# FFN-down of a hybrid decoder layer: 29 of 64 squares by seven products instead of 22, with the weight sums of 15 of them made ahead and kept in DRAM

## The chip, the cores and the metric

The kernel runs on one core of one Trainium2 chip. The metric is the device time of one execution in microseconds. Five engines matter: TensorE (PE, with its weight loads as PEld), VectorE (DVE), ScalarE (ACT), GpSimd (POOL) and SyncE (SP). SP computes nothing here; it issues nearly all DMAs, in order, and waits on semaphores.

## The reference, cut to what matters

The whole layer has 256 tokens and a width of 2048. The change touches only the channel mixer:

```python
h2 = rms_norm(x, mlp_norm[i])                                          # 256 x 2048
x = x + jnp.square(jax.nn.relu(h2 @ w_ffn_up[i])) @ w_ffn_down[i]      # 2048 -> 8192 -> 2048
gate = jax.nn.sigmoid(rms_norm(x, ple_norm[i]) @ w_ple_gate[i])        # comes next
```

All of it is float32. `w_ffn_up` and `w_ffn_down` have 64 MB each and are read once from DRAM.

## The kernel before, in words

**Precision.** Every float32 operand is split into a high part (rounded to `fp32r` by an ACT copy) and a low part (the rest, by a DVE subtraction). A product is then three matmuls: high by high, high by low, low by high. For a weight tile of 128x1024, `halves_of` (L1115 ff.) issues two ACT copies of 128x512 (L1122) and one DVE subtraction of 128x1024 (L1123). `split_sb` (L154, L155) does the same for one 128x512 block.

**Order in time.** `ffn_half(0)` and `ffn_half(1)` follow each other. Each one runs eight `gemm_wide` (the up half: 1024 of the 8192 hidden columns at a time in two `half` steps of 256 columns, 64 loads of 512 KB per up half) and then two `down_sweep`s, one for each `pair` (1024 of the 2048 output columns). A sweep goes over 16 values of `kp`; each is a "square": 256 hidden rows by 1024 output columns, by 256 tokens. Two halves, two sweeps and 16 squares make 64 squares.

**A square.** Its weights are two loads of 512 KB, `rx` and `ry`. With 128x512 blocks b11, b12 (`rx`) and b21, b22 (`ry`) and 128x128 blocks of activations a11 to a22, the plain form has eight block products of three matmuls each: 24 matmuls. The other form (`kp in seven`) is Winograd's with seven products: 21 matmuls, but it needs sums of the activations (`activation_sums`, made in the up half and kept in the `S` tiles) and sums of the weights. The weight sums t1, t3, t2, t4 are four DVE operations of 128x512 (L1151 to L1154) inside the sweep, into the tile `td` of slot `a1`, and are then split like weights. Before the change the seven-product squares are kp 1, 3, 6, 8, 11, 13, and only 1, 3, 6, 11 in the last sweep: 3 x 6 + 4 = 22.

**Buffers.** The pool `wp` has three slots of each of three tags: `raw` (what a DMA writes, 512 KB), `wh` and `wl` (the split halves that PE reads). All weight loads of the kernel share the three `raw` slots through `load_raw` (L138 to L140). The fourth split tile of a seven-product square is taken from the tag `graw` of the pool `fp`. `keep` loads four tiles of the gate weights in the last sweep (`graw` too), and the row of the final norm (`fn`) goes into slot `a0` when that is free.

**Who sets the order.** The code is written as a data flow. A scheduler in the compiler sets each engine's order of instructions before the run, by priority (program order, and ahead of it what stands in `tc.high_priority`) among the instructions whose inputs and slots are there by its own account. At run time each engine and SP's queue then go through that fixed order, and wait where they must.

Of the kernel before, what the change touches and what calls it, by code (L numbers as in the profile page):

```python
# [9 lines left out]
F32 = mybir.dt.float32  # L10
F32R = mybir.dt.float32r
AF = mybir.ActivationFunctionType
ALU = mybir.AluOpType
# [27 lines left out]
def trunk(  # L41
# [23 lines left out]
    act = ctx.enter_context(tc.tile_pool(name="act", bufs=1))  # L65
    psm = ctx.enter_context(tc.tile_pool(name="psm", bufs=4, space=PSUM))
    rctx = ctx.enter_context(ExitStack())
    psr = rctx.enter_context(tc.tile_pool(name="psr", bufs=4, space=PSUM))

    def mm_bank(name):  # L70
# [20 lines left out]
    make_identity(nc, ident)  # L91
    ones = const.tile([128, 128], F32, name="ones")
    nc.vector.memset(ones, 1.0)
    jsum = const.tile([128, 128], F32, name="jsum")
    cmask = const.tile([128, 128], F32, name="cmask")
    rmask = const.tile([128, T], F32, name="rmask")
    sbd = [const.tile([128, 4, 128], F32, name=f"sbd{i}") for i in range(2)]
    make_block_diagonal(nc, cmask, 64)
    nc.gpsimd.tensor_copy(jsum, cmask)
    cen = const.tile([128, 128], F32, name="cen")  # L100
    nc.vector.scalar_tensor_tensor(cen, jsum, -1.0 / 64.0, ident, op0=ALU.mult, op1=ALU.add)
    jhead = const.tile([128, 2], F32, name="jhead")
    nc.gpsimd.tensor_copy(jhead, cmask[:, ::64])
    for r0 in (0, 64):
        make_upper_triangular(nc, cmask[r0 : r0 + 64, 0:64], val=1.0, diag=False)
# [2 lines left out]
    nc.gpsimd.memset(rmask.rearrange("p (c t) -> p c t", t=64)[:, :, 0:1], 0.0)  # L108
    for i in range(2):
        nc.vector.memset(sbd[i], 0.0)  # L110
    edge = const.tile([128, 4, 16], F32, name="edge")
    nc.vector.memset(edge, 1.0)
    for g, win in enumerate(WINDOWS):
        for t in range(win - 1):
            nc.gpsimd.memset(edge[:, g, t : t + 1], float(win) / (t + 1))


    wband = const.tile([128, 4, 272], F32, name="wband")

    def make_bands():  # L120
        for g, win in enumerate(WINDOWS):
# [6 lines left out]
            nc.vector.tensor_tensor(w0[:, 0:128], w0[:, 0:128], ident, op=ALU.subtract)  # L128

    m0, m1 = PARAM_COLS["mu_r"], PARAM_COLS["mu_wag"] + 3  # L130
    omu = const.tile([128, m1 - m0], F32, name="omu")
    nc.vector.tensor_scalar(omu, par_sb[:, m0:m1], -1.0, 1.0, op0=ALU.mult, op1=ALU.add)
    oka = const.tile([128, 8], F32, name="oka")
# [4 lines left out]
    def load_raw(src, n, name):  # L138
        raw = wp.tile([128, 1024], F32, tag="raw", name=f"raw_{name}")
        nc.sync.dma_start(raw[:, 0:n], src)  # L140
        return raw
# [11 lines left out]
    def split_sb(h_ap, l_ap, src_ap):  # L153
        nc.scalar.activation(h_ap, src_ap, AF.Copy)  # L154
        nc.vector.tensor_tensor(l_ap, src_ap, h_ap.bitcast(F32), op=ALU.subtract)  # L155
# [93 lines left out]
    def a8(slot, name, dt=F32):  # L249
        return act.tile([128, 2048], dt, tag=f"a{slot}", name=name)  # L250
# [36 lines left out]
    hsel = const.tile([8, 512], F32R, name="hsel")  # L287
    nc.gpsimd.tensor_copy(hsel, hsel_f)

    def flat(t_):  # L290
# [89 lines left out]
    normed(0)  # L380
    normed(1)

    zf = const.tile([128, 3, T], F32, name="zf")
    zwa, zg, zg2 = zf[:, 0], zf[:, 1], zf[0:64, 2]

    def wag_out():
# [681 lines left out]

    SEVEN = (1, 3, 6, 8, 11, 13)
    s_slots = (0, 2, 5)

    def activation_sums(box, kp, r):

        i = SEVEN.index(kp)
        if i % 2 == 0:
            box[kp] = box[SEVEN[min(i + 1, len(SEVEN) - 1)]] = a8(s_slots[i // 2], f"S{kp}", F32R)
        st = box[kp][:, i % 2 * 1024 : i % 2 * 1024 + 1024]
        t_ = fp.tile([128, 1024], F32, tag="junk", bufs=1, name=f"s{kp}")  # L1080
        s1, s2_, s3, s4 = (t_[:, j * 128 : (j + 1) * 128] for j in range(4))
        a11, a21, a12, a22 = (r[:, j * 128 : (j + 1) * 128] for j in range(4))
        nc.vector.tensor_tensor(s1, a21, a22, op=ALU.add)
        nc.vector.tensor_tensor(s3, a11, a21, op=ALU.subtract)
        nc.vector.tensor_tensor(s2_, s1, a11, op=ALU.subtract)
        nc.vector.tensor_tensor(s4, a12, s2_, op=ALU.subtract)
        split_sb(st[:, 0:512], st[:, 512:1024], t_[:, 0:512])

    def down_sweep(hf, pair, ys, sboxes, hooks=(), between=None, seven=SEVEN):
# [43 lines left out]
        for q, kp in enumerate((0, 2, 1, 4, 3, *range(5, 16)) if pair else range(16)):  # L1133
            if q in hooks:
                hooks[q]()
            y, j = ys[kp // 2], kp % 2 * 512
            a11, a21, a12, a22 = ((y[:, j + i * 128 : j + i * 128 + 128], y[:, 1024 + j + i * 128 : 1152 + j + i * 128]) for i in range(4))
            rx, ry = (load_raw(w_down[pair, hf * 32 + 2 * kp + i], 1024, f"{nm}_{kp}_{i}") for i in range(2))
            if kp in seven:
                i = SEVEN.index(kp)  # L1140
                st = sboxes[kp][:, i % 2 * 1024 : i % 2 * 1024 + 1024]
                s1, s2_, s3, s4 = ((st[:, c * 128 : c * 128 + 128], st[:, 512 + c * 128 : 640 + c * 128]) for c in range(4))
                t_ = a8(1, f"t{nm}_{kp}")
                t1, t3, t2, t4 = (t_[:, c * 512 : c * 512 + 512] for c in range(4))
                wa = fp.tile([128, 1024], F32R, tag="wa", name=f"wa{nm}_{kp}")
                w11 = wa[:, 0:512], wa[:, 512:1024]
                with tc.high_priority(20000):
                    split_sb(*w11, rx[:, 0:512])
                w21, w22 = halves_of(ry, f"{nm}_{kp}b")
                with tc.high_priority(20000):  # L1150
                    nc.vector.tensor_tensor(t1, rx[:, 512:1024], rx[:, 0:512], op=ALU.subtract)  # L1151
                    nc.vector.tensor_tensor(t3, ry[:, 512:1024], rx[:, 512:1024], op=ALU.subtract)
                    nc.vector.tensor_tensor(t2, t3, rx[:, 0:512], op=ALU.add)
                    nc.vector.tensor_tensor(t4, ry[:, 0:512], t2, op=ALU.subtract)  # L1154
# [28 lines left out]
    def ffn_half(hf):  # L1183
        sboxes = {}
        ys = []
        for i in range(8):
            f = hf * 8 + i
            y = fp.tile([128, 2048], F32R, tag="y", bufs=8, name=f"y{f}")

            def square(bi, bank):  # L1190
                r = fp.tile([128, 512], F32, tag="r", bufs=2, name=f"r{f}_{bi}")
                r2 = r.rearrange("p (c t) -> p c t", c=2)
                nc.scalar.activation(r2, bank[:, :, T : 2 * T], AF.Copy)
                nc.vector.tensor_tensor(r2, bank[:, :, 0:T], r2, op=ALU.add)
                nc.vector.scalar_tensor_tensor(r, r, 0.0, r, op0=ALU.max, op1=ALU.mult)
                split_sb(y[:, bi * 512 : bi * 512 + 512], y[:, 1024 + bi * 512 : 1024 + bi * 512 + 512], r)
                if 2 * i + bi in SEVEN:
                    activation_sums(sboxes, 2 * i + bi, r)

            gemm_wide(w_up[f], h2, f"u{f}", square)  # L1200
            ys.append(y)
            if f == 1:
                inv_ms()

        if hf == 1:
            h3_part, h3 = transposed("h3")
            h3_box.append(h3)

        down_sweep(hf, 0, ys, sboxes)
        if hf == 0:  # L1210
            down_sweep(hf, 1, ys, sboxes)
        else:
            down_sweep(hf, 1, ys, sboxes, {5: keep, 8: keep, 11: keep, 14: keep}, lambda: [h3_part("ple_norm", n) for n in range(2)], (1, 3, 6, 11))
            for n in range(2, 4):
                h3_part("ple_norm", n)

# [149 lines left out]
```

## Time and profile before

| | us |
|---|---|
| median of 3 runs (lowest, highest) | 1203.55 (1201.89, 1203.93) |
| the profiled execution's own time | 1201.35 |
| its span in the profile | 1199.6 |

The mean granted TensorE clock of the profiled execution is 0.997. Its span lies 1.75 us under its own time, and its own time 2.2 us under the median. In the profile's rows, a group of instructions is given as line, engine, operation, what it writes and reads, count, busy time, and mean nanoseconds of one. `raw_d` are the loads of `w_ffn_down`, `raw_u` those of `w_ffn_up`; `d_b` and `d_w` are the PSUM banks of the down product, `u_w` of the up product; `wh_d_12a` and `wl_d_12a` are the split halves of a square's first load (kp 12), `b` the second, `c` and `d` the weight sums; `wad` is the split b11 block. A matmul's duration in a row is longer than its distance to the next, since matmuls are pipelined.

### The profile page before, as it was taken

The numbers are of one execution on the slowest core, as the hardware profiler recorded it, in microseconds if no ns is written. First come the engines' busy times: TensorE is split into PE (matmuls) and PEld (weight loads), VectorE is DVE, ScalarE is ACT, GpSimd is POOL, SyncE is SP. The second block draws the span as 40 slices with busy tenths as digits, with TensorE's granted clock in tenths as the row PEclk, the third lists the DMA queues.
The fourth block names the chain that finished last, engine by engine and source line by source line (L and its number), as shares of the span: only waits on it lengthen the run. The fifth ranks groups of instructions, "written<-read, shape, count | busy, mean of one in ns | idle before, by whom it ended". The sixth has DMA issues, their size and how long they took to land.

```text
span 1199.6 us, 18428 instructions
## 1 busy us (share of the span) xinstructions
PE 1179.5 (98%) x7060; PEld 1010.6 (84%) x7060; DVE 868.5 (72%) x1149; ACT 689.8 (58%) x1276; POOL 18.1 (2%) x69
## 2 busy tenths in 40 slices
PE   8999999999999999999999999999999999999997
PEld 6999988987887888888888788888888888777886
DVE  7687987965656666666878888666667879787552
ACT  6857566566545565555655564454555555668544
POOL 4000010000000000000000000000000000000000
PEclk9999999999999999999999999999999999999999
DMA  6463542354445555555665656655555556766531
GB/s 246 154 201 109 175 144 104 113 198 141 140 163 179 184 185 190 192 191 189 201 201 200 193 195 211 191 181 188 189 184 189 207 194 197 287 231 211 195 120 70
DMA packets 60328, 216.88 MB, mean 181 GB/s; under 512 B 6736, under 2 KB 7120, under 8 KB 59856
## 3 DMA queue, kind: packets, MB, share of 16 engines
q1 hardware_dynamic: 59952, 215.19, 53.4%
q8 instruction: 55, 0.90, 0.3%
q10 hardware_dynamic: 288, 0.52, 0.1%
q14 instruction: 33, 0.27, 0.1%
HBM read 213.59 MB, written 2.10 MB: 180 GB/s over the span
## 4 chain that ended last, share of the span: by engine, by line
PE 81%; DVE 8%; DMA 4%; ACT 4%; issue 2%; SPq 0%; ACTq 0%; DVEq 0%
PE u_w L997 20%; PE u_w L1001 10%; PE d_b L1112 5%; PE d_b L1113 5%; PE d_b L1111 5%; DMA raw_d<-in_w_ffn_down_dram 3%; PE gt_b L171 2%; PE gt_b L173 2%; PE gt_b L172 2%; PE wag_b L331 1%; PE zp_b L171 1%; PE o_b L171 1%; PE o_b L172 1%; PE o_b L173 1%; PE d_w L1112 1%
## 5 line engine op out<-in xcount | busy, mean ns | idle before, releaser
L997 PE MATMUL u_w<-h,wh_u 128*128 128x512 f32 x1024 | 358.8, 395 | 0.0
L1001 PE MATMUL u_w<-h,wl_u 128*128 128x256 f32 x1024 | 287.3, 281 | 0.0
L149 ACT ACTIVATE wh_u<-raw_u 128x512 fp32r<-128x512 f32 x256 | 147.6, 624 | 166.2 <-PE u_w L997 93.1
L150 DVE TENSOR_TENSOR wl_u<-raw_u,wh_u 128x1024 fp32r<-128x1024 f32 x128 | 156.7, 1225 | 115.1 <-ACT wh_u L149 115.1
L997 PEld LDWEIGHTS u_w<-h,wh_u 128*128 128x128 f32 x1024 | 192.0, 187 | 44.8
L1001 PEld LDWEIGHTS u_w<-h,wl_u 128*128 128x128 f32 x1024 | 193.6, 189 | 0.0
L150 DVE TENSOR_TENSOR wl_gt<-raw_gt,wh_gt 128x1024 fp32r<-128x1024 f32 x24 | 29.4, 1225 | 23.9 <-ACT wh_gt L149 23.9
L149 ACT ACTIVATE wh_gt<-raw_gt 128x512 fp32r<-128x512 f32 x48 | 27.8, 631 | 23.0 <-PE gt_b L173 18.8
L1151 DVE TENSOR_TENSOR td<-raw_d 128x512 f32<-128x512 f32 x22 | 15.2, 693 | 31.0 <-DMA raw_d<-in_w_ffn_down_dram 31.0
L162 PE MATMUL zv_b<-hTh,wh_zv 128*128 128x256 f32 x128 | 37.6, 294 | 0.0
L171 PE MATMUL gt_b<-wh_gt,h 128*128 128x512 f32 x96 | 37.5, 390 | 0.0
L162 PE MATMUL zr_b<-hTh,wh_zr 128*128 128x256 f32 x128 | 37.4, 292 | 0.0
L173 PE MATMUL gt_b<-wh_gt,h 128*128 128x512 f32 x96 | 37.4, 389 | 0.0
L172 PE MATMUL gt_b<-wl_gt,h 128*128 128x512 f32 x96 | 37.4, 389 | 0.0
L164 PE MATMUL zr_b<-hTh,wl_zr 128*128 128x256 f32 x128 | 37.0, 289 | 0.1
L163 PE MATMUL zr_b<-hTl,wh_zr 128*128 128x256 f32 x128 | 37.0, 289 | 0.0
L162 PE MATMUL zk_b<-hTh,wh_zk 128*128 128x256 f32 x128 | 36.9, 288 | 0.0
L163 PE MATMUL zk_b<-hTl,wh_zk 128*128 128x256 f32 x128 | 36.3, 284 | 0.5 <-DVE hTl L155 0.5
L164 PE MATMUL zk_b<-hTh,wl_zk 128*128 128x256 f32 x128 | 36.3, 284 | 0.1
L163 PE MATMUL zv_b<-hTl,wh_zv 128*128 128x256 f32 x128 | 36.2, 283 | 0.0
L164 PE MATMUL zv_b<-hTh,wl_zv 128*128 128x256 f32 x128 | 36.2, 283 | 0.0
L154 ACT ACTIVATE wad<-raw_d 128x512 fp32r<-128x512 f32 x22 | 13.9, 632 | 33.7 <-DMA raw_d<-in_w_ffn_down_dram 29.1
(807 smaller groups left out, 3077.6 us busy)
## 6 DMA issues: line engine op xcount, KB each, us to landing
raw_u<-in_w_ffn_up_dram SPq DMA_DIRECT2D x128, 512.0 KB, 3.6
raw_d<-in_w_ffn_down_dram SPq DMA_DIRECT2D x128, 512.0 KB, 4.0
raw_gt<-in_w_ple_gate_dram SPq DMA_DIRECT2D x24, 512.0 KB, 3.5
raw_zk<-in_w_in_dram SPq DMA_DIRECT2D x16, 512.0 KB, 3.3
raw_zr<-in_w_in_dram SPq DMA_DIRECT2D x16, 512.0 KB, 3.4
raw_zv<-in_w_in_dram SPq DMA_DIRECT2D x16, 512.0 KB, 3.2
raw_zp<-in_w_in_dram SPq DMA_DIRECT2D x16, 512.0 KB, 3.3
raw_o<-in_w_out_dram SPq DMA_DIRECT2D x16, 512.0 KB, 3.5
```

What stands on the lines that cost most here:

```text
L149: nc.scalar.activation(wh[:, a * 512 : (a + 1) * 512], raw[:, a * 512 : (a + 1) * 512], AF.Copy)
L150: nc.vector.tensor_tensor(wl, raw, wh.bitcast(F32), op=ALU.subtract)
L162: nc.tensor.matmul(o, w_h, ah, start=first and ct % 2 == 0, stop=False, skip_group_check=True)
L163: nc.tensor.matmul(o, w_h, al, start=False, stop=False, skip_group_check=True)
L164: nc.tensor.matmul(o, w_l, ah, start=False, stop=last, skip_group_check=True)
L171: nc.tensor.matmul(o, a_h, wh[:, 0:n], start=first, stop=False)
L172: nc.tensor.matmul(o, a_h, wl[:, 0:n], start=False, stop=False)
L173: nc.tensor.matmul(o, a_l, wh[:, 0:n], start=False, stop=last)
L997: nc.tensor.matmul(bank[:, ct, :].rearrange("p (s t) -> p s t", s=2), wh[:, c], hl, start=k == 0, stop=False, skip_group_check=True,)
L1001: nc.tensor.matmul(bank[:, ct, 0:T], wl[:, c], hl[:, 0, :], start=False, stop=k == 15, skip_group_check=True)
L1111: nc.tensor.matmul(banks[n], ah, wh, start=first, stop=False)
L1112: nc.tensor.matmul(banks[n], ah, wl, start=False, stop=False)
```

## The change

More squares take the seven-product form: kp 1, 3, 5, 7, 9, 11, 12, 13 in three sweeps and 1, 3, 7, 9, 11 in the last, 3 x 8 + 5 = 29. Of these, the squares with kp 3, 7, 11, 13 (3, 7, 11 in the last sweep), 15 in all, get their weight sums ahead of time: `ahead` loads both weight tiles in the up half before (2 x 512 KB), makes the four sums there with four DVE operations in place, and writes the 1 MB tile (t2, t1, t4, t3 in the places of b11, b12, b21, b22) to a DRAM scratch tensor `sums{n}`. The tile is in slot `a1` for odd n and in a new single slot `pr` for even n. The store of one tile is written in the code after the next `gemm_wide`.

In the sweep such a square reads four times instead of twice: 256 KB of `rx` (b11 alone), `ry`, and the two halves of the stored tile, all through the `raw` slots, and makes no sums. The other seven-product squares stay as they were. Two more pairs of activation sums are made per half, and a new tile `S` holds them. Constants that only the mixer needs move from the pool `const` to a pool `mixc` that is closed before the FFN, which gives the room for `pr` and `S`.

```diff
-    SEVEN = (1, 3, 6, 8, 11, 13)
+    SEVEN = (1, 3, 5, 7, 9, 11, 12, 13)
+    AHEAD = (3, 7, 11, 13)
+    LAST = (1, 3, 7, 9, 11)
     s_slots = (0, 2, 5)
+    sums = {}
+
+    def ahead(hf, pair, kp, n):
+        t_ = a8(1, f"pr{n}") if n % 2 else fp.tile([128, 2048], F32, tag="pr", name=f"pr{n}")
+        for i in range(2):
+            nc.sync.dma_start(t_[:, i * 1024 : (i + 1) * 1024], w_down[pair, hf * 32 + 2 * kp + i])
+        b11, b12, b21, b22 = (t_[:, c * 512 : c * 512 + 512] for c in range(4))
+        nc.vector.tensor_tensor(b22, b22, b12, op=ALU.subtract)
+        nc.vector.tensor_tensor(b12, b12, b11, op=ALU.subtract)
+        nc.vector.tensor_tensor(b11, b22, b11, op=ALU.add)
+        nc.vector.tensor_tensor(b21, b21, b11, op=ALU.subtract)
+        d = dram.tile([128, 2048], F32, name=f"sums{n}")
+        sums[hf, pair, kp] = d
+        return lambda: nc.sync.dma_start(d, t_)
...
-            rx, ry = (load_raw(w_down[pair, hf * 32 + 2 * kp + i], 1024, f"{nm}_{kp}_{i}") for i in range(2))
+            pre = kp in seven and sums.get((hf, pair, kp))
+            rx, ry = (
+                load_raw(w_down[pair, hf * 32 + 2 * kp + i][:, 0:n], n, f"{nm}_{kp}_{i}")
+                for i, n in enumerate((512 if pre else 1024, 1024))
+            )
...
+            if pre:
+                ra, rb = (load_raw(pre[:, c * 1024 : c * 1024 + 1024], 1024, f"{nm}_{kp}_t{c}") for c in range(2))
+                wa = fp.tile([128, 1024], F32R, tag="wa", name=f"wa{nm}_{kp}")
+                w11 = wa[:, 0:512], wa[:, 512:1024]
+                with tc.high_priority(20000):
+                    split_sb(*w11, rx[:, 0:512])
+                w21, w22 = halves_of(ry, f"{nm}_{kp}b")
+                w2, w1 = halves_of(ra, f"{nm}_{kp}c")
+                w4, w3 = halves_of(rb, f"{nm}_{kp}d", True)
+                for n, a_, w_ in (("1", a11, w11), ("2", a12, w21), ("3", s4, w22), ("5", s1, w1), ("6", s2_, w2), ("7", s3, w3), ("4", a22, w4)):
+                    prod(n, a_, w_)
+            elif kp in seven:
...
+        plan = [(pair, kp) for pair in range(2) for kp in AHEAD if kp in LAST or not (hf and pair)]
+        store = None
         for i in range(8):
             f = hf * 8 + i
+            stored, store = store, ahead(hf, *plan[i], hf * 8 + i) if i < len(plan) else None
...
             gemm_wide(w_up[f], h2, f"u{f}", square)
+            if stored is not None:
+                stored()
```

More of the change, by code (lines that the diff above doesn't have):

```diff
@@ L67, in trunk @@
     rctx = ctx.enter_context(ExitStack())
+    mixc = rctx.enter_context(tc.tile_pool(name="mixc", bufs=1))
+    dram = ctx.enter_context(tc.tile_pool(name="sums", bufs=1, space=bass.MemoryType.DRAM))
     psr = rctx.enter_context(tc.tile_pool(name="psr", bufs=4, space=PSUM))
@@ L93, in trunk @@
     nc.vector.memset(ones, 1.0)
[L94 to L97, printed above, removed]
+    jsum = mixc.tile([128, 128], F32, name="jsum")
+    cmask = mixc.tile([128, 128], F32, name="cmask")
+    rmask = mixc.tile([128, T], F32, name="rmask")
+    sbd = [mixc.tile([128, 4, 128], F32, name=f"sbd{i}") for i in range(2)]
     make_block_diagonal(nc, cmask, 64)
     nc.gpsimd.tensor_copy(jsum, cmask)
-    cen = const.tile([128, 128], F32, name="cen")
+    cen = mixc.tile([128, 128], F32, name="cen")
     nc.vector.scalar_tensor_tensor(cen, jsum, -1.0 / 64.0, ident, op0=ALU.mult, op1=ALU.add)
-    jhead = const.tile([128, 2], F32, name="jhead")
+    jhead = mixc.tile([128, 2], F32, name="jhead")
     nc.gpsimd.tensor_copy(jhead, cmask[:, ::64])
@@ L110, in trunk @@
         nc.vector.memset(sbd[i], 0.0)
-    edge = const.tile([128, 4, 16], F32, name="edge")
+    edge = mixc.tile([128, 4, 16], F32, name="edge")
     nc.vector.memset(edge, 1.0)
@@ L115, in trunk @@
             nc.gpsimd.memset(edge[:, g, t : t + 1], float(win) / (t + 1))
-    wband = const.tile([128, 4, 272], F32, name="wband")
+    wband = mixc.tile([128, 4, 272], F32, name="wband")
     def make_bands():
@@ L130, in trunk @@
     m0, m1 = PARAM_COLS["mu_r"], PARAM_COLS["mu_wag"] + 3
-    omu = const.tile([128, m1 - m0], F32, name="omu")
+    omu = mixc.tile([128, m1 - m0], F32, name="omu")
     nc.vector.tensor_scalar(omu, par_sb[:, m0:m1], -1.0, 1.0, op0=ALU.mult, op1=ALU.add)
-    oka = const.tile([128, 8], F32, name="oka")
+    oka = mixc.tile([128, 8], F32, name="oka")
     ka0 = PARAM_COLS["k_a"]
@@ L286, in trunk @@
     nc.gpsimd.affine_select(hsel_f, hsel_f, [[-1, 512]], ALU.is_ge, 0.0, base=63, channel_multiplier=64)
-    hsel = const.tile([8, 512], F32R, name="hsel")
+    hsel = mixc.tile([8, 512], F32R, name="hsel")
     nc.gpsimd.tensor_copy(hsel, hsel_f)
@@ L381, in trunk @@
     normed(1)
-    zf = const.tile([128, 3, T], F32, name="zf")
+    zf = mixc.tile([128, 3, T], F32, name="zf")
     zwa, zg, zg2 = zf[:, 0], zf[:, 1], zf[0:64, 2]
@@ L1077, in activation_sums @@
         if i % 2 == 0:
-            box[kp] = box[SEVEN[min(i + 1, len(SEVEN) - 1)]] = a8(s_slots[i // 2], f"S{kp}", F32R)
+            st = a8(s_slots[i // 2], f"S{kp}", F32R) if i < 6 else fp.tile([128, 2048], F32R, tag="S", name=f"S{kp}")
+            box[kp] = box[SEVEN[min(i + 1, len(SEVEN) - 1)]] = st
         st = box[kp][:, i % 2 * 1024 : i % 2 * 1024 + 1024]
@@ L1203, in ffn_half @@
                 inv_ms()
+        if store is not None:
+            store()
         if hf == 1:
@@ L1212, in ffn_half @@
         else:
-            down_sweep(hf, 1, ys, sboxes, {5: keep, 8: keep, 11: keep, 14: keep}, lambda: [h3_part("ple_norm", n) for n in range(2)], (1, 3, 6, 11))
+            down_sweep(hf, 1, ys, sboxes, {5: keep, 8: keep, 11: keep, 14: keep}, lambda: [h3_part("ple_norm", n) for n in range(2)], LAST)
             for n in range(2, 4):
```

## The prediction

> **What bounds the kernel now.** I read the page first, then windows of 20 us over the FFN.
>
> ```profile
> span 1199.6 us, 18428 instructions
> PE 1179.5 (98%) x7060; PEld 1010.6 (84%) x7060; DVE 868.5 (72%) x1149; ACT 689.8 (58%) x1276; POOL 18.1 (2%) x69
> 600.00:620.00 20.00, 20.00 (x90) 16.54 (x90) 14.66 (x16) 10.28 (x18) 0.00 (x0) 1.00 0.65 206
> 780.00:800.00 20.00, 20.00 (x115) 17.34 (x114) 13.91 (x18) 10.77 (x20) 0.00 (x0) 1.00 0.58 184
> 1020.00:1040.00 20.00, 20.00 (x88) 16.19 (x87) 16.12 (x16) 11.49 (x20) 0.00 (x0) 1.00 0.78 286
> 1040.00:1060.00 20.00, 19.21 (x85) 15.60 (x84) 15.56 (x16) 13.23 (x23) 0.00 (x0) 1.00 0.71 255
> ```
>
> PE is busy almost all the time, in a down sweep (600), in an up half (780), at the granted clock 1.00. The last columns are the DMA share and GB/s. In the last sweep (1040), where more is loaded, PE first loses something. The timeline of PE gives the stages by their first matmuls (167.56 us for the two sweeps of the first half, of which 83.00 for the first), and the spacing of matmuls from the first of a plain square to the first of the next:
>
> ```profile
> 567.13 0.39 PE L1111 MATMUL d_b<-wh_d_0a,y 128*128 128x512 f32 x1
> 629.05 0.39 PE L1111 MATMUL d_b<-wh_d_12a,y 128*128 128x512 f32 x1
> 634.49 0.39 PE L1111 MATMUL d_w<-wad,y 128*128 128x512 f32 x1
> 650.13 0.39 PE L1111 MATMUL d_b<-wh_d_0a,y 128*128 128x512 f32 x1
> 734.69 0.39 PE L997 MATMUL u_w<-h,wh_u 128*128 128x512 f32 x1
> 915.58 0.40 PE L1111 MATMUL d_b<-wh_d_0a,y 128*128 128x512 f32 x1
> 998.67 0.47 PE L1111 MATMUL d_b<-wh_d_0a,y 128*128 128x512 f32 x1
> 1088.10 0.28 PE L1018 MATMUL h3t<-ident,x 128*128 128x128 f32 x1
> ```
>
> From 629.05 to 634.49 lie 24 matmuls: 0.2267 us each, not the 0.39 of a row. A sweep of ten plain and six seven-product squares has 366 matmuls, 82.97 us. The four sweeps took 83.00, 84.56, 83.09 and 89.43 us, so the first and third run at PE's pace and the others lose a little. How near the supply is to its limit is seen in what ACT and DVE waited for, and in the landing times of loads:
>
> ```profile
> DVE td L1151 <- DMA raw_d<-in_w_ffn_down_dram: 31.0, 20, 3.2
> ACT wad L154 <- DMA raw_d<-in_w_ffn_down_dram: 29.1, 18, 3.0
> SPq L140 <- DVE td L1153: 21.7, 12, 4.1
> DMA to landing us min/median/max: 3.3/3.9/5.1
> DMA packets 8819, 32.16 MB, mean 201 GB/s; under 512 B 987, under 2 KB 987, under 8 KB 8810
> raw_d<-in_w_ffn_down_dram SPq DMA_DIRECT2D x59, 512.0 KB, 3.9
> raw_d<-in_w_ffn_down_dram SPq DMA_DIRECT2D x8, 512.0 KB, 5.5
> ```
>
> Every seven-product square begins with ACT and DVE waiting for its weights, and the queue of SP waits for DVE to free a `raw` slot (the first two rows are of 380 to 1090 us, SP's of 560 to 740). The lines on landing: first half's sweeps (570 to 730, 201 GB/s) 3.9 us, and 5.5 us in 1020 to 1040, where `fn` and `graw` came on top (286 GB/s, the row at 1020 above). A sweep is thus PE-bound with a chain "slot free, load, split, slot free" close behind it. That chain is what the change loads.
>
> **The change: what it takes from PE.** Seven squares lose three matmuls each: 7 x 3 x 0.2267 = 4.76 us. This counts only where PE sets the pace.
>
> **The change: the ring of three raw slots.** A slot's time is landing plus holding. The holding, from rows of two neighbouring squares (12 plain, 13 seven-product):
>
> ```profile
> 624.95 1.15 ACT L1122 ACTIVATE wh_d_12a<-raw_d 128x512 fp32r<-128x512 f32 x2 [0.24 <-DMA raw_d<-in_w_ffn_down_dram]
> 626.32 1.22 DVE L1123 TENSOR_TENSOR wl_d_12a<-raw_d,wh_d_12a 128x1024 fp32r<-128x1024 f32 x1
> 628.75 0.63 ACT L154 ACTIVATE wad<-raw_d 128x512 fp32r<-128x512 f32 x1 [2.65 <-DMA raw_d<-in_w_ffn_down_dram]
> 629.42 0.69 DVE L155 TENSOR_TENSOR wad<-raw_d,wad 128x512 fp32r<-128x512 f32 x1
> 631.03 1.16 ACT L1122 ACTIVATE wh_d_13b<-raw_d 128x512 fp32r<-128x512 f32 x2 [0.60 <-DMA raw_d<-in_w_ffn_down_dram]
> 632.32 0.69 DVE L1153 TENSOR_TENSOR td<-td,raw_d 128x512 f32<-128x512 f32 x1
> 634.07 0.69 DVE L1154 TENSOR_TENSOR td<-raw_d,td 128x512 f32<-128x512 f32 x1
> raw_pT<-in_pT_dram SPq DMA_DIRECT2D x1, 256.0 KB, 3.5
> ```
>
> A plain tile is held from 624.95 to 627.54, 2.6 us: with 3.9 to land, 6.5. A square with sums in the sweep holds `rx` from 628.75 to the end of t2, 633.01 (4.3), and `ry` from 631.03 to the end of t4, 634.76 (3.7): 8.2 + 7.6 = 15.8. A square with sums made ahead has no row; it is built of them: `rx` of 256 KB lands in 3.5 (the only load of that size without company, `pT`) and is held for 0.63 + 0.69, so 4.8; three tiles like plain ones make 19.5; together 24.3, half as much again as the square it replaces.
>
> Before, a sweep needs 10 x 13.0 + 6 x 15.8 = 224.8 slot-us, over three slots 74.9 us, under PE's 83.0. After, kp goes plain, sums, plain, ahead, four times per sweep: 13.0 + 15.8 + 13.0 + 24.3 = 66.1 slot-us, 22.0 us over three slots, and PE needs 90 x 0.2267 = 20.4. The ring becomes the bound: 4 x 22.0 = 88.1 us per sweep. That holds for 3.9 us of landing. The sweep reads 16.78 + 4 x 0.79 = 19.9 MB, at 88.1 us 226 GB/s; between (201 GB/s, 3.9) and (286, 5.5) on a line, and let settle, landing goes to about 4.2 and the sweep to 92. I take 90, the middle: 3 x 90 against the 250.65 measured is **+19.4 us**. Ends: PE's 81.6 a sweep (-5.9 in all, if landing is under 3.36, where nine full loads with 0.54 less each take 66.1 to 61.2), and 96 (+37, if landing is 4.5).
>
> The Trainium skill, "DMA: Bandwidth & Descriptors", section on the anatomy of one DMA, fits a transfer as 2.0 us plus its bytes at 436 GB/s, for another issuing path than SP's. By that, an estimate: 512 KB lands in 3.2 us, the ring is under PE's pace and the sum would be -4.8 instead of +19.4. The median of 59 loads here is 3.9 and the least 3.3, so I go by the rows.
>
> DVE gains in the sweep: a square with sums costs it 0.69 + 3 x 1.22 + 4 x 0.69 = 7.1 us, one ahead 4.4, a plain one 2.4; per sweep 4 x 7.1 + 4 x 4.4 + 8 x 2.4 = 65 against 6 x 7.1 + 10 x 2.4 = 67. It does not bind, and what it saves is on an engine that waited for DMA anyway. ACT has seven copies of about 0.6 us in the one form and four in the other: 82 copies before, 88 after, some 53 of 82 us. The new order of products 5, 6, 7 costs nothing.
>
> **The last sweep.** Five such squares instead of four, three of them ahead: 369 matmuls, -0.68 us. Its ring goes from 12 x 13.0 + 4 x 15.8 = 219.2 to 11 x 13.0 + 2 x 15.8 + 3 x 24.3 = 247.5, 73.1 to 82.5 us, under PE's 83.7 at 3.9 us, but here landing was 5.5 for a stretch. It lost 89.43 - 372 x 0.2267 = 5.1 us before, transposes of h3 in it. I take **+3**, bounds -0.7 and +12.6 (the 9.4, and six more loads with 1.6 more each over three slots).
>
> **The up halves.** Each of the 15 tiles adds two loads of 512 KB, four DVE operations (2.8 us, in an engine busy 13.9 of 20) and a store of 1 MB, on the same SP queue; up to 2.1 MB per `gemm_wide` of 22.6 us (180.9 us from 734.69 to 915.58, over eight), from 184 to 277 GB/s. Nearest rows:
>
> ```profile
> raw_u<-in_w_ffn_up_dram SPq DMA_DIRECT2D x57, 512.0 KB, 4.3
> graw<-in_w_ple_gate_dram SPq DMA_DIRECT2D x2, 512.0 KB, 6.9
> fn<-in_final_norm_dram SPq DMA_DIRECT2D x1, 1024.0 KB, 5.4
> out_dram<-x SPq DMA_DIRECT2D x4, 384.0 KB, 2.9
> 1024.24 0.33 SPq L1234 DMA_DIRECT2D fn<-in_final_norm_dram  x1
> ```
>
> An up load has 3 x 180.9 / 64 = 8.5 us for landing and holding. It uses 4.3 + 2.6 = 6.9, and with 5.5 of landing 8.1: just hidden. But `fn`, written in the code after the whole FFN, was issued at 1024, when its slot came free. The new loads and stores may likewise go early and close together. At 6.9 us of landing, the longest of these rows (`graw`, 1050 to 1070), the ring would need 3.17 us per load instead of 2.83; over some 30 loads 10 us. I take **+2**, bounds 0 and +10. The added activation sums (two more per half) lie on DVE and ACT in the same cover. The move of constants to another pool changes no instruction, 0.
>
> Sum: 1201.35 + 19.4 + 3 + 2 = 1225.8, **1226 us** (the median of the runs is 2.2 above the profiled execution; I make nothing of that).
>
> **The rivals.** *PE keeps the pace* (faster). If loads land in under 3.36 us, all sweeps run at 0.2267 per matmul: 1201.35 - 4.8 = 1196.6, or 1195 with the 1.6 us that the second sweep lost. For it: single loads land in 3.3, and in 1025 to 1030 the engines moved 388 GB/s, so bandwidth isn't used up.
>
> ```profile
> 1025.00:1030.00 5.00, 5.00 (x24) 4.14 (x23) 4.56 (x6) 2.56 (x5) 0.00 (x0) 1.00 0.97 388
> ```
>
> Against it: what limits is three slots, and their landing was 3.9 with less in flight. The Trainium skill, same page, specifications, gives about 358 GB/s as a core's share of HBM, of which 244 (19.9 MB in PE's 81.6 us) would be two thirds; by that rule this rival is right. Chance 0.15.
>
> *Partly hidden*: landing 3.4 to 3.6 and quiet up halves give 1199 to 1208. Chance 0.08.
>
> *SP's queue is blocked in the up half.* The load of a tile's next contents waits on its slot until the store before it has landed, about 5.4 us by `fn`, and the `raw_u` loads are queued behind it; then ACT and DVE wait, then PE. The margin is 8.5 - 6.9 = 1.6 us plus two split tiles ahead of PE, 2 x 2.83 less the 2.6 of a split, 4.7 in all. If the order puts reload right after store, 13 reloads cost 0.7 us each, and with the two loads of the reload in front of `raw_u` (2 x 1.6, the 512 KB step from 3.9 to 5.5) 3.9 each: 1235 to 1277 with the ring. For it: SP goes through one fixed order. Against: the store (2.9 us for 384 KB at the end of the kernel) is short beside the time between tiles. It decides only where the wait is over 4.7 us. Chance 0.07.
>
> **How the numbers follow.** The ring as bound, 1208 to 1245: 0.70. A measurement of this kernel can tell about 0.2% (2.4 us) from no change. Faster by more than that: 0.15. Within it: 0.05, from the partly hidden case. Slower: 0.80. The range 1202 to 1245 leaves out the faster rival and the worst of the blocked queue.
>
> **What would show it.** In the sweeps: PE at 18 to 19 of 20 instead of 20.00, more waits of ACT and DVE on `raw_d`, DMA above 215 GB/s, first to last matmul of a full sweep near 90 us, landing about 4.2. In the up halves: `u_w` at full pace, 181 us for the second. If a full sweep takes 81.6 to 82 us, the ring arithmetic is wrong; if the up halves grow by over 10 us, the loss lies elsewhere than I say.

## The result, and the profile after

The changed kernel takes 1253.77 us (median of 5 runs, 1248.55 to 1258.15), the kernel before 1201.89 us in the runs beside it (1199.8 to 1203.93): 1.0444 times as long, 95% interval 1.0419 to 1.0468. It is slower, as forecast, but by 52 us instead of 24. The profiled execution took 1248.55 us, with a span of 1246.5 us, 46.9 us over the span before. The other 5 us of the median lie in executions without a profile; their granted clock is 0.987 to 0.993, that of the profiled one 0.995.

The page of the changed kernel, and windows of 20 us in two full sweeps, the last sweep and the two up halves (columns as before: PE, PEld, DVE, ACT, POOL, granted clock, DMA share, GB/s):

```profile
span 1246.5 us, 18626 instructions
PE 1200.3 (96%) x7039; PEld 1002.8 (80%) x7039; DVE 901.7 (72%) x1211; ACT 703.8 (56%) x1301; POOL 18.2 (1%) x69
...
raw_d_t<-sums SPq DMA_DIRECT2D x30, 512.0 KB, 5.3
```
```profile
400.00:420.00 20.00, 20.00 (x115) 17.38 (x114) 16.11 (x22) 10.20 (x18) 0.00 (x0) 1.00 0.91 323
620.00:640.00 20.00, 17.45 (x69) 12.38 (x68) 13.66 (x16) 10.60 (x20) 0.00 (x0) 1.00 0.57 185
720.00:740.00 20.00, 16.91 (x66) 12.13 (x65) 13.22 (x15) 9.59 (x17) 0.00 (x0) 0.97 0.63 182
860.00:880.00 20.00, 20.00 (x115) 17.36 (x114) 12.56 (x14) 10.34 (x20) 0.00 (x0) 1.00 0.57 186
1060.00:1080.00 20.00, 17.61 (x71) 12.63 (x69) 9.35 (x9) 9.02 (x16) 0.00 (x0) 1.00 0.74 273
```

In these windows of the sweeps PE starts 66 to 71 matmuls in 20 us instead of 90. These are among the slowest. The next rows are the three full sweeps as a whole, and last the first sweep of the kernel before:

```profile
569.73:663.23 93.50, 87.25 (x362) 66.31 (x361) 68.44 (x75) 51.01 (x90) 0.00 (x0) 1.00 0.66 208
663.23:762.91 99.68, 89.82 (x361) 67.40 (x361) 70.21 (x77) 50.40 (x89) 0.00 (x0) 0.98 0.65 211
943.80:1036.54 92.74, 87.14 (x362) 66.37 (x361) 68.37 (x75) 50.86 (x90) 0.00 (x0) 1.00 0.66 210
567.13:650.13 83.00, 83.00 (x368) 68.70 (x367) 70.15 (x80) 47.81 (x84) 0.00 (x0) 1.00 0.60 198
```

PE is busy 18.0 to 18.8 us of 20, and the DMA engines move 208 to 211 GB/s instead of 198. In the up half, with the loads ahead on top (323 GB/s), PE is full. The total of 96% hides that: a busy PE counts its modelled ends, so the count of matmuls says more than the busy time. The lower granted clock of the second sweep (0.98) is not what makes it the longest: `raw_spaced`, below, has a second sweep of 99.9 us at 1.00.

The stages from the timeline of PE:

```profile
388.00 0.47 PE L999 MATMUL u_w<-h,wh_u 128*128 128x512 f32 x1
569.73 0.40 PE L1131 MATMUL d_b<-wh_d_0a,y 128*128 128x512 f32 x1
663.23 0.47 PE L1131 MATMUL d_b<-wh_d_0a,y 128*128 128x512 f32 x1
762.91 0.39 PE L999 MATMUL u_w<-h,wh_u 128*128 128x512 f32 x1
943.80 0.40 PE L1131 MATMUL d_b<-wh_d_0a,y 128*128 128x512 f32 x1
1036.54 0.39 PE L1131 MATMUL d_b<-wh_d_0a,y 128*128 128x512 f32 x1
1149.89 0.39 PE L173 MATMUL gt_b<-wh_gt,h 128*128 128x512 f32 x1
```

The kernel before has its first up matmul at 388.74 and the first one of the gate that follows the FFN at 1102.67. From these:

| stage, us | before | after | difference |
|---|---|---|---|
| start to first up matmul | 388.7 | 388.0 | -0.7 |
| up half 0, up half 1 | 178.4, 180.9 | 181.7, 180.9 | +3.3, 0 |
| full sweeps | 83.0, 84.6, 83.1 | 93.5, 99.7, 92.7 | **+35.3** |
| last sweep, to the gate | 104.0 | 113.4 | +9.4 |

The loss is in the sweeps. There the chain that ended last, for a stretch with one square whose sums were made ahead (kp 7), goes mostly through loads (columns: start, duration, what):

```profile
600.70 3.54 DMA raw_d<-in_w_ffn_down_dram
...
604.35 1.16 ACT wh_d_7b L1142 x2
605.51 0.02 issue
605.53 1.24 DVE wl_d_7b L1143
606.77 0.02 issue
606.78 4.31 DMA raw_d<-in_w_ffn_down_dram
...
611.20 1.16 ACT wh_d_8a L1142 x2
612.36 0.02 issue
612.38 1.24 DVE wl_d_8a L1143
613.62 0.02 issue
613.63 4.48 DMA raw_d<-in_w_ffn_down_dram
```

Each load is issued 0.01 us after a subtraction has freed its slot, lands, is split, and so frees the slot for the next: the ring is full, and PE isn't on the path. The timeline of SP and DVE around the same square shows what holds the slots:

```profile
600.70 0.33 SPq L142 DMA_DIRECT2D raw_d<-in_w_ffn_down_dram  x1
602.27 1.28 SPq L142 DMA_DIRECT2D raw_d_t<-sums  x2
605.53 1.23 DVE L1143 TENSOR_TENSOR wl_d_7b<-raw_d,wh_d_7b 128x1024 fp32r<-128x1024 f32 x1 [2.34 <-ACT wh_d_7b L1142]
609.12 1.23 DVE L1143 TENSOR_TENSOR wl_d_7c<-raw_d_t,wh_d_7c 128x1024 fp32r<-128x1024 f32 x1 [2.36 <-ACT wh_d_7c L1142]
610.28 1.23 DVE L1143 TENSOR_TENSOR wl_d_7d<-raw_d_t,wh_d_7d 128x1024 fp32r<-128x1024 f32 x1
```

From 603.2 to 606.8 all three slots are in use by `ry` and the two reloads, and nothing can be issued. The two reloads, issued 0.9 us apart, take 5.6 and 5.8 us to land (the DMA views of 601.5 to 602.6 and of 603.0 to 603.6, one load in each):

```profile
raw_d_t<-sums SPq DMA_DIRECT2D x1, 512.0 KB, 5.6
...
raw_d_t<-sums SPq DMA_DIRECT2D x1, 512.0 KB, 5.8
```

DVE stands idle twice for 2.3 us meanwhile. Median landing in the sweeps of the first half (570 to 765):

```profile
raw_d<-in_w_ffn_down_dram SPq DMA_DIRECT2D x51, 512.0 KB, 4.1
raw_d_t<-sums SPq DMA_DIRECT2D x16, 512.0 KB, 5.8
raw_d<-in_w_ffn_down_dram SPq DMA_DIRECT2D x8, 256.0 KB, 3.1
```

### The profile page after: what moved, and what is told of

It reads as the page before. It is cut to its first block, busy times and chain, and to the rows that moved or that the text cites. A ratio compares the mean times of both kernels' runs of the same rounds, so it can differ in the third digit from the quotient of the medians.

```text
span 1246.5 us, 18626 instructions
## 1 busy us (share of the span) xinstructions
PE 1200.3 (96%) x7039; PEld 1002.8 (80%) x7039; DVE 901.7 (72%) x1211; ACT 703.8 (56%) x1301; POOL 18.2 (1%) x69
## 4 chain that ended last, share of the span: by engine, by line
PE 71%; DMA 11%; DVE 11%; ACT 4%; issue 3%; SPq 0%; ACTq 0%; DVEq 0%
PE u_w L999 19%; PE u_w L1003 10%; DMA raw_d<-in_w_ffn_down_dram 6%; PE d_b L1132 3%; DMA raw_d_t<-sums 3%; PE d_b L1133 3%; PE d_b L1131 3%; PE gt_b L173 2%; PE gt_b L175 2%; PE gt_b L174 2%; PE zp_b L173 1%; PE zp_b L175 1%; PE zp_b L174 1%; PE zv_b L164 1%; DVE X L625 1%
## 5 line engine op out<-in xcount | busy, mean ns | idle before, releaser
L151 ACT ACTIVATE wh_o<-raw_o 128x512 fp32r<-128x512 f32 x32 | 18.4, 624 | 19.6 <-PE o_b L175 10.1
L156 ACT ACTIVATE wad<-raw_d 128x512 fp32r<-128x512 f32 x29 | 18.2, 629 | 16.7 <-DMA raw_d<-in_w_ffn_down_dram 16.3
```

Of the source, the lines that this page charges most:

```text
L151: nc.scalar.activation(wh[:, a * 512 : (a + 1) * 512], raw[:, a * 512 : (a + 1) * 512], AF.Copy)
```

## The experiments

The theory was that of the prediction: the three `raw` slots set the pace, and the two reloads per square ahead are what overloads them. Rivals: reads of the scratch tensor are slow; the seven-product form itself costs more than it saves; the work in the up halves is the loss. Ratios are to the kernel before in runs of the same batch; the changed kernel's is 1.0444. The sweeps named are the three full ones.

**The slots alone.** `two_slots` is the kernel before with two slots for `raw`.

```diff
-        raw = wp.tile([128, 1024], F32, tag="raw", ...)
+        raw = wp.tile([128, 1024], F32, tag="raw", bufs=2, ...)
```

> The kernel before with two raw slots in place of three, nothing else: a test of the slot arithmetic where the change plays no part. Theory: a full sweep takes 224.8 / 2 = 112 us in place of 83, an up half 64 x (3.5 to 4.3 + 2.6) / 2 = 195 to 221 in place of 180; total 1330 to 1430. Rival (slots hardly matter, waits overlap): sweeps under 95 us, total under 1260.

Measured: 1372.4 us in one run. The first two sweeps, from the rows:

```profile
594.97 0.39 PE L1111 MATMUL d_b<-wh_d_0a,y 128*128 128x512 f32 x1
...
812.59 0.39 PE L997 MATMUL u_w<-h,wh_u 128*128 128x512 f32 x1
```

217.6 us, 108.8 each. With 3.6 us of landing the sum of the prediction gives (224.8 - 32 x 0.3) / 2 = 107.6; the loads of these two sweeps land in 3.5 (median) to 3.8 us (mean), for which it gives 106 to 110. Plain tiles are held 2.5 to 2.9 us there and the two of a square with sums 4.4 and 3.3, where 2.6, 4.3 and 3.7 were priced. The up halves, 196.8 and 211.2 us, also lie in the theory's 195 to 221. So slot times from single rows, added up and divided by the number of slots, give the length of a stage whose ring is the bound, here within 3%.

`six_slots` goes the other way: the squares of the kernel before, with three more slots, for each square's second load. It is made from the changed kernel, so the constants are moved as there.

```diff
+    def load_own(src, name):
+        raw = fp.tile([128, 1024], F32, tag="raw2", bufs=3, name=f"raw2_{name}")
...
+                load_raw(...) if i == 0 else load_own(...)
```

> The kernel before (22 squares) with three slots more for the second load of each square in the sweeps, in the room that the moved constants leave. Theory: the sweeps that lost something (84.56 and 89.43 us) run at PE's pace, full sweeps 83.0: 1197 to 1200. Rival (DVE sets these losses, not the slots): 1200 to 1203, no change.

Measured: 1202.35 us (1201.13 to 1204.47), ratio 1.0016 (0.9999 to 1.0033), sweeps 83.6, 83.5, 83.3. Before the change the ring was not the bound; more slots win 0.3 us in the three sweeps together.

**The reloads out of the ring.** `own_slot` is the changed kernel with the sums coming back by one load of 1 MB into the slot `pr`.

```diff
-                ra, rb = (load_raw(pre[:, c * 1024 : c * 1024 + 1024], 1024, ...) for c in range(2))
+                rs_ = fp.tile([128, 2048], F32, tag="pr", ...)
+                nc.sync.dma_start(rs_, pre)
+                ra, rb = rs_[:, 0:1024], rs_[:, 1024:2048]
```

> The changed kernel, but in an ahead square the stored sums come back with one load of 1 MB into the slot pr, which stands empty in the sweeps, instead of two loads of 512 KB through the three raw slots. The bytes, the products and the work in the up halves are the same. Theory (three raw slots are the bound): an ahead square then takes 4.8 + 6.5 = 11.3 slot-us, a group of four squares 53.1, 17.7 us over three slots, under PE's 20.4: full sweeps of 82 to 85 us, total 1197 to 1208. Rival (the added bytes, or slow reads of the scratch tensor, are the bound whatever slot they go to): sweeps stay above 92 us, total above 1240.

Measured: 1212.61 us (1205.61 to 1215.46), ratio 1.0095 (1.0057 to 1.0133), sweeps 86.0, 83.7, 85.1. Two neighbouring windows:

```profile
600.00:620.00 20.00, 20.00 (x90) 16.57 (x89) 13.71 (x15) 10.66 (x20) 0.00 (x0) 1.00 0.71 222
620.00:640.00 20.00, 18.04 (x78) 14.16 (x77) 15.96 (x18) 10.98 (x20) 0.00 (x0) 1.00 0.63 215
```

The same bytes, stores and sums, and PE is at 90 matmuls again at 600: of the 4.4% some 3.5 lay in the passage through `raw`. It didn't go as low as the theory's 1197 to 1208.

`half_own` sends only the second reload through `pr`.

```diff
+                ra = load_raw(pre[:, 0:1024], 1024, ...)
+                rb = fp.tile([128, 2048], F32, tag="pr", ...)[:, 0:1024]
+                nc.sync.dma_start(rb, pre[:, 1024:2048])
```

> The changed kernel, but of the two loads that bring back the stored sums one goes through the raw slots as before and the other into the slot pr. Theory (three raw slots, with a threshold where their arithmetic crosses PE's): an ahead square takes 4.8 + 6.5 + 6.5 = 17.8 slot-us, a group 59.6, 19.9 us, just under PE's 20.4, so near the run with both in the slot pr: 1210 to 1222. Rival (each load costs its share, with no threshold): half way between that run's 1212.6 and the changed kernel's 1253.8, 1233.

Measured: 1227.18 us (1222.84 to 1228.11), ratio 1.0213 (1.0176 to 1.025), sweeps 88.8, 91.7, 86.9. It lies between what the two theories gave: one load less in the ring takes away about half of the loss (2.3 of the 4.4%).

**Is it the scratch tensor, or the work ahead?** `weights_read` reads two weight tiles in place of the stored sums; `weights_read_no_up` makes nothing ahead either.

```diff
-                ra, rb = (load_raw(pre[:, c * 1024 : c * 1024 + 1024], 1024, ...) for c in range(2))
+                ra, rb = (load_raw(w_down[pair, hf * 32 + 2 * kp + c], 1024, ...) for c in range(2))
...
+        sums.update({(hf, *p): True for p in plan})    # weights_read_no_up only: the squares stay marked
+        plan = []                                      # weights_read_no_up only
```

> The changed kernel, but the two loads of an ahead square that read the stored sums read two weight tiles instead (same bytes, same raw slots, rows without gaps; the result is then not the reference's). Sums are still made and stored in the up halves. Theory (raw slots alone): the loads land late because they come close together, so landing stays near 5 us and the total at 1240 to 1254. Rival (the scratch tensor is slow to read): these loads land in 3.7 to 4.1 like the other weights, sweeps fall to 88 to 91 us, total 1225 to 1235.

> As the run that reads weights in place of the sums, and the up halves do nothing ahead: no loads, sums or stores there (the result is not the reference's). What it is faster than that run is the price of the work in the up halves: by the trace of the changed kernel about 3 us, the first up half having grown from 178.4 to 181.7 us. Rival (stores and loads ahead also disturb the sweeps): 10 us or more.

Measured: 1250.3 us (1248.05 to 1250.51), ratio 1.0413 (1.0391 to 1.0436), and 1240.95 us (1238.98 to 1242.76), ratio 1.0339 (1.0314 to 1.0365). In the first, 570 to 765:

```profile
raw_d_t<-in_w_ffn_down_dram SPq DMA_DIRECT2D x16, 512.0 KB, 4.7
```

The reloads of weights land after 4.7 us, those of sums after 5.8, and the sweeps are hardly shorter (92.1, 100.2, 94.2). Reads of the scratch tensor do land later, but that is worth about 0.3% of the 4.4%, and the two intervals overlap: the rival that these reads are the loss falls. The 9.4 us between the two kernels are about what the work ahead costs while the ring is the bound. Some 3 of them are a second up half of 177.5 us (last section), and 3.6 a second sweep of 96.6 instead of 100.2 us: the first loads ahead for the second half are issued at its end (at 741.4 and 746.6 in the changed kernel).

`up_only` asks the same from the other side: the sweeps of before, and the loads, sums and stores of 15 squares in the up halves, not used by anyone.

```diff
-    SEVEN = (1, 3, 5, 7, 9, 11, 12, 13)
+    SEVEN = (1, 3, 6, 8, 11, 13)        # AHEAD (3, 6, 11, 13), LAST (1, 3, 6, 11)
...
+            pre = None
```

> The sweeps of the kernel before (22 squares, all sums in the sweep), while the up halves load 15 squares, make their sums and store them as in the changed kernel; nothing reads the stored sums. This is the price of the work ahead alone. Theory: what it costs is at the edges (bunched loads before the first up half, loads for the second in the sweep before it), as the two runs that read weights differ by 9.4 us with and without it: 1206 to 1212. Rival (it is free, and the 9.4 us came from something else): 1200 to 1203.

Measured: 1204.75 us (1202.93 to 1208.48), ratio 1.0033 (1.0015 to 1.0051): about 4 us, between the two expectations. In its trace 3.3 of them are a first up half of 181.7 instead of 178.4 us (last section); the full sweeps take 83.0, 83.8 and 83.0.

`none_ahead` makes all sums of the 29 squares in the sweeps, with no scratch tensor.

```diff
+        plan = []
```

> 29 squares by seven products, none with sums made ahead: all weight sums in the sweep, no scratch tensor, nothing added to the up halves. Theory (raw slots): a group is 13.0 + 15.8 + 13.0 + 15.8 = 57.6 slot-us, 19.2 us, under PE's 20.4, and DVE has 19.0 of 20.4: sweeps of 83 to 87 us, total 1200 to 1215, so well under the changed kernel. Rival (more seven-product squares are what costs, through DVE and ACT): at least as slow as the changed kernel, 1250 or more.

Measured: 1214.06 us (1210.95 to 1215.11), ratio 1.0107 (1.008 to 1.0134), sweeps 85.6, 88.9, 85.1: the upper end of the theory's 1200 to 1215, with one sweep over its 87. So the seven more squares alone do not pay either. Where PE starts only 75 matmuls, DVE is busy 19.28 of 20:

```profile
980.00:1000.00 20.00, 18.16 (x75) 13.17 (x74) 19.28 (x24) 12.38 (x22) 0.00 (x0) 1.00 0.52 158
```

That DVE sets the pace here is likely from this row, but no run tests it.

**What else is in the ring's time?** `half_reload` keeps the changed kernel's loads, but a reload brings 256 KB.

```diff
-                ra, rb = (load_raw(pre[:, c * 1024 : c * 1024 + 1024], 1024, ...) for c in range(2))
+                ra, rb = (load_raw(pre[:, c * 1024 : c * 1024 + 512], 512, ...) for c in range(2))
```

> The changed kernel, but each reload from the scratch tensor brings 256 KB instead of 512 KB (the first 512 columns of the tile), and the copies and subtractions of that tile use these columns twice, so two of the four weight sums are left out. Slots, copies, matmuls and the order of the loads stay; two subtractions of 128x512 stand for one of 128x1024, 0.16 us more holding. Theory (the ring of three slots is the bound and the reloads' landing of 5.3 to 5.8 us is the term that was taken too short): these land in 3.1 to 3.6 us, a group of four squares needs 4 to 5 slot-us less, so each full sweep is 5 to 7 us shorter (87 to 91 us instead of 93.5, 99.7 and 92.8), and the total 1228 to 1238 us. Rival (the excess over the slot sum comes from the number of loads and the fixed order of SP's queue, whatever their landing): less than 6 us is won, 1246 us or more.

Measured: 1242.23 us (1241.87 to 1243.16), ratio 1.0364 (1.034 to 1.0389), sweeps 91.3, 96.9, 91.2. Landing, 570 to 765:

```profile
raw_d<-in_w_ffn_down_dram SPq DMA_DIRECT2D x52, 512.0 KB, 3.6
raw_d_t<-sums SPq DMA_DIRECT2D x16, 256.0 KB, 3.9
```

The landing of the reloads fell from 5.8 to 3.9 us (3.1 to 3.6 were expected), the time by 0.8% (some 10 us) instead of the theory's 16 to 26. So landing is a part only. `raw_spaced` tries whether it is the two squares ahead that stand close together (kp 11 and 13): 26 squares, with four between any two ahead.

```diff
-    SEVEN, AHEAD = (1, 3, 5, 7, 9, 11, 12, 13), (3, 7, 11, 13)
+    SEVEN, AHEAD = (1, 3, 5, 7, 9, 11, 13), (1, 5, 9, 13)      # LAST = (1, 3, 5, 9, 11)
```

> The changed kernel with the 26 squares of own_spaced (kp 1, 5, 9, 13 ahead, 3, 7, 11 with sums in the sweep), the reloads through the raw slots as in the changed kernel. Slot sum with the changed kernel's landing times (4.1, 3.1, 5.8): 9 plain, 3 with sums, 4 ahead need 281 slot-us, 93.6 us a sweep, against 94.5 for the changed kernel's mix. Theory (the sum of slot times sets the sweep, whatever the spacing): sweeps 1 to 3 us shorter than the changed kernel's, 1244 to 1252 us. Rival (the changed kernel loses above the slot sum because kp 11 and 13 stand close together): sweeps near 90 us, 1230 to 1238 us.

Measured: 1248.96 us (1244.1 to 1252.32), ratio 1.0406 (1.0365 to 1.0446), sweeps 93.2, 99.9, 93.5, as the theory had it. Spacing wins nothing. Where the time goes is seen from the issue and the landing of each load. The slots rotate, so a load's slot is free again when the third load after it is issued; the difference less the landing is the holding. Means over 78 loads of the first two sweeps, by kind, worked out from the DMA views of single loads:

| slot time (landing + holding), us | priced | changed kernel | `half_reload` | `ahead_only` |
|---|---|---|---|---|
| plain square, first load, after a square with sums | 6.5 | 8.7 (4.1 + 4.6) | 8.2 (3.6 + 4.6) | none |
| plain square, first load, otherwise | 6.5 | 7.1 (4.3 + 2.8) | 6.8 (4.2 + 2.6) | 7.0 (4.2 + 2.7) |
| plain square, second load | 6.5 | 6.9 (4.1 + 2.9) | 7.3 (4.0 + 3.2) | 7.2 (4.3 + 2.9) |
| square with sums, both | 15.8 | 15.4 | 15.6 | none |
| ahead: `rx`; after a square with sums | 4.8; 4.8 | 5.5; 8.4 | 5.6; 9.6 | 6.0; none |
| ahead: `ry` | 6.5 | 6.2 (3.7 + 2.5) | 6.2 | 6.1 |
| ahead: the two reloads | 13.0 | 16.2 (11.1 + 5.1) | 13.9 (8.0 + 5.9) | 14.4 (9.4 + 5.0) |

That such slot times, over three slots, give the sweep is so by construction, as they run from issue to issue; those of the kernel before give 84.2 and 84.6 us for its 83.0 and 84.6, though PE is its bound. What the table shows is where the time lies. That the ring is the bound here is seen elsewhere: a reload or `ry` is split within 0.1 us of its landing, where a plain square's second load waits 1.1 us on average in the kernel before; and `own_slot` gives the time back.

The first row is seen on DVE's timeline behind the square with sums kp 9:

```profile
619.59 0.69 DVE L1190 TENSOR_TENSOR td<-raw_d,td 128x512 f32<-128x512 f32 x1
620.20 1.22 DVE L1143 TENSOR_TENSOR wl_d_9b<-raw_d,wh_d_9b 128x1024 fp32r<-128x1024 f32 x1
621.34 1.22 DVE L1143 TENSOR_TENSOR wl_d_9c<-td,wh_d_9c 128x1024 fp32r<-128x1024 f32 x1
622.47 1.22 DVE L1143 TENSOR_TENSOR wl_d_9d<-td,wh_d_9d 128x1024 fp32r<-128x1024 f32 x1
623.61 1.22 DVE L1143 TENSOR_TENSOR wl_d_10a<-raw_d,wh_d_10a 128x1024 fp32r<-128x1024 f32 x1
```

The first load of kp 10 landed at 620.5, but its slot is freed at 624.8: DVE first does the three subtractions of kp 9. To test that, `ahead_only` keeps the 15 squares ahead and makes the other 14 plain, so that no sums are made in the sweep and PE has 12 more matmuls in each.

```diff
+        seven = tuple(k for k in seven if (hf, pair, k) in sums)
```

> The changed kernel with its 15 squares whose sums are made ahead, but the 14 squares that make their sums in the sweep take the plain form: 12 plain and 4 ahead per full sweep. Theory (in the changed kernel a plain tile that follows a square with sums is held 4.6 us instead of 2.8, since its subtraction stands behind that square's sums on DVE; this is 2 to 3 us a sweep): without sums in the sweep all plain tiles are held about 2.8; 24 x (4.15 + 2.8) + 4 x 28 = 279 slot-us, 93 us a sweep in the first half against 96.6 on average now, though PE has 12 matmuls (2.7 us) more to do; total 1240 to 1246. Rival (the long holding is PE's back pressure or lies in the ring itself): sweeps as long as now or longer by PE's 2.7 us each, 1253 to 1262.

Measured: 1232.88 us (1227.46 to 1234.73), ratio 1.0245 (1.0215 to 1.0276).

```profile
573.37 0.40 PE L1132 MATMUL d_b<-wh_d_0a,y 128*128 128x512 f32 x1
662.79 0.47 PE L1132 MATMUL d_b<-wh_d_0a,y 128*128 128x512 f32 x1 [0.39 <-DVE x L1152]
755.29 0.39 PE L999 MATMUL u_w<-h,wh_u 128*128 128x512 f32 x1
```

89.4 and 92.5 us in the first half, against 93.5 and 99.7, with more work for PE. The plain tiles are held 2.7 to 2.9 us, the theory's 2.8, and the reloads land earlier as well (4.5 and 4.9 instead of 5.2 and 5.9), which the theory had not said; that is likely why the time fell below its 1240. The slot times are 12 x 14.14 + 4 x 26.46 = 275.5, 91.8 us over three slots, and 91.0 is the mean measured. The third sweep, 92.2 against 92.7, hardly moved: the long holding is gone there too (4.7 to 2.9 us), but other loads take longer, and its slot times fall only from 286.6 to 281.5, 1.7 us over three slots.

**Towards a better version.** `own_spaced` is `own_slot` with the 26 squares of `raw_spaced`, so that `pr` is free in time; `own_spaced_late` also holds back the first two tiles ahead until the FFN begins.

```diff
+        if n < 2:                                                   # own_spaced_late only
+            for i in range(2):
+                nc.vector.tensor_copy(t_[:, i * 1024 : i * 1024 + 256], h2(15)[:, 0, :].bitcast(F32))
```

> As own_slot (the stored sums come back by one 1 MB load into slot pr, past the raw slots), but 26 squares by seven products: kp 1, 3, 5, 7, 9, 11, 13, of them 1, 5, 9, 13 with sums made ahead, so that four squares lie between two of these; in the last sweep 1, 3, 5, 9, 11. Theory (the 1 to 3 us that each sweep of own_slot still loses come from kp 11 and 13, whose reloads wait for the one slot pr): four squares are over 20 us apart, pr is free again in time, and each full sweep takes PE's pace, 363 x 0.2267 = 82.3 us (82 to 84); gt_b starts 3 to 5 us earlier against the first up matmul than in own_slot; with own_slot's start, 3.5 us late, 1203 to 1208. Rival (the rest comes from the order of DVE's and SP's work in the sweep, not from that spacing): sweeps of 84 to 86 us and 1210 to 1214.

> As own_spaced, and the loads of the first two tiles ahead are made to wait for h2 (a small DVE copy of h2 into the tile ahead of its load), so that they don't run in the stage before the FFN. Theory (own_slot started its first up matmul 3.5 us late because these loads crowded that stage): the first up matmul goes back to 388 to 390 us and the total is 2 to 3.5 us under own_spaced, 1200 to 1205, no slower than the kernel before. Rival (the start is late for another reason, or the crowd just moves into the up half): the same as own_spaced within 1 us, or slower.

Measured: 1210.11 us (1207.75 to 1216.88), ratio 1.0106 (1.0079 to 1.0133), sweeps 82.3, 87.4, 84.1; and 1213.6 us (1205.47 to 1218.16), ratio 1.0116 (1.0085 to 1.0148), sweeps 88.6, 85.6, 85.9 in an execution of 1218.16. Both theories fell. The first sweep of `own_spaced` is at PE's 363 x 0.2267 = 82.3, but not the second. The first up matmul is at 389.5 in both, so `own_slot`'s 392.2 wasn't due to those loads. No version beat the kernel before; the nearest that uses the sums ahead lie 1% above it. Of the 1% of `own_spaced`, some 12 us, about 4 are what `up_only` costs too and 3 lie in the full sweeps (253.8 against 250.7); the rest is open.

## Why the prediction was right in kind and wrong in size

- *"The ring becomes the bound"*: right. `two_slots` shows the sum at work, `six_slots` that the ring wasn't the bound before, `own_slot` that taking the reloads out gives back 3.5 of 4.4%. PE's 4.76 us were not to be had, as said.
- *A full sweep of 90 us, +19.4*: wrong; 93.5, 99.7 and 92.7, +35.3. This is the step that failed: the slot time of the ring, by two of its terms, landing and holding, and some small change. The working itself came to 92 (+25) with its settled landing; that 90, the middle, was taken had no row behind it. By the table, a sweep of the first half needs 293 slot-us (97.7 us over three slots; 96.6 is the mean measured) where 264.4 were priced (88.1); a square ahead needs 28.6 instead of 24.3. Of the 28.6 between the two sums, the landing of the reloads, 5.2 and 5.9 for 3.9, makes 4 x 3.3 = 13.4. I had asked what landing would be at 226 GB/s on average; but the reloads are issued close together, and 5.5 for a crowded stretch stood in my rows. These shares don't come off one by one: `half_reload` took 12.6 slot-us of landing away, 4.2 us a sweep, and the sweeps were 1.5 to 2.8 us shorter, as other loads, and the reloads themselves, were held longer.
- *"It does not bind"*, of DVE: wrong where it mattered. 65 us of work in 88 says nothing of the few us behind a square with sums. There the holding is 4.6 instead of 2.6 for three plain tiles and 4.5 instead of 1.3 for the `rx` of kp 13: 6.0 + 3.2 = 9.2 slot-us. The 2.6 came from a tile (kp 12 of before) whose copies ended at 626.1, when DVE was nearly through with the square ahead of it (626.3). The remaining 6.0 are the other plain tiles, with up to 4.3 of landing and 2.9 of holding, and `rx`, held 2.2 instead of 1.3, less what `ry` and the squares with sums fell short.
- *The last sweep, +3*: +9.4, inside the bounds of -0.7 and 12.6. It is presumably for the same reasons, which no run shows for this sweep by itself; the ring was "under PE's 83.7" only at 3.9 us.
- *The up halves, +2*: near, by luck. The loads did go early (323 GB/s at 400), and the cover of 8.5 us per load held, as PE kept 115 matmuls in 20 us. The +3.3 and 0 have another source: kernels without any work ahead have the 3.3 too (last section). Blocking of SP's queue there did not come. What the prediction put at nothing are the loads ahead for the second half that are issued in the sweep before it: 3.6 us between the two runs that read weights.
- *PE keeps the pace*: fell. The fit of the Trainium skill ("DMA: Bandwidth & Descriptors", anatomy of one DMA), made for another issuing path than SP's, gives by estimate 3.2 us for 512 KB. The shortest landing among the loads behind the table is 3.3, but the two of a pair take 5.2 and 5.9 on average: the trace does not agree where loads come together. The same page of the Trainium skill (specifications) has about 358 GB/s as a core's limit of HBM, and by that the sweeps should have kept PE's pace. They moved 208 to 211 GB/s, and those of `own_slot`, which are shorter, 229 to 251: the ring, not the memory, sets the pace.
- *What would show it*: 18 to 19 of 20 for PE came as 18.0 to 18.8 over a sweep, the second up half as 180.9 us. "DMA above 215 GB/s" did not come, with 208 to 211, because the sweeps took longer than 90 us; the landing of 4.2 came for the weights (4.1) and not for the reloads.

`six_slots`, with the constants moved and no work ahead, is within 0.2% of the kernel before. That the new order of products costs nothing, no run shows by itself.

## What to carry to other kernels

Where a few slots in rotation feed the bottleneck, add up landing plus holding of every load and divide by the slots: it gave 107.6 for 108.8 us in `two_slots`. But take landing from loads issued as close together as the new ones will be, and holding from a tile that queues behind the longest work of the engine that frees it. Work that is moved ahead still loads the ring that it was to relieve if its result comes back by the same slots; give it a slot of its own, and then compare with what the saving is worth.

## What the runs showed that I had not expected

An up half runs at one of two paces: 117 to 118 matmuls in 20 us (178 us in all) or 115 (181 us), at a granted clock shown as 1.00 in both. The kernel before has the one in its first half (at 400) and the other in its second (x115 at 780):

```profile
400.00:420.00 20.00, 20.00 (x117) 17.66 (x116) 13.85 (x19) 10.62 (x19) 0.00 (x0) 1.00 0.61 192
```

The work ahead does not choose the pace: `none_ahead` and `six_slots`, which load nothing ahead, have 115 at 400 and 181.7 us in the first half, and in `own_slot` it changes within a half (x115 at 400, x118 at 480). So the +3.3 us of the changed kernel's first up half is this step and not the price of the loads. But the kernel before, with its one trace, is the only one that begins its first half at 117; the changed kernel and the twelve made from it all begin it at 115. Whether something that these share, such as the moved constants, sets it there is not known.
